# A two-layer decoder trunk on one core: most tile transposes go from TensorE to VectorE and a crossing through memory

## The chip, the core and the metric

The kernel runs on one core of a Trainium2 chip. A core has TensorE (PE), VectorE (DVE), ScalarE (ACT), GpSimd (POOL) and SyncE (SP), each with an instruction queue of its own that it works through in order, and 16 DMA engines. The metric is device time in microseconds. The profile's "span" is the time from the first to the last recorded work of one execution.

## What is computed

Two decoder layers on 256 tokens of width 2048, in float32. In each layer the input projection has seven parts (q, k, v, g_att, glu_a, glu_b, g_conv); one head group does attention, the other a convolution module, and one output projection brings both back to the residual stream.

```python
def conformer_conv(glu_a, glu_b, dw_kernel, dw_bias, ln_g, ln_b, w_pw):
    u = glu_a * jax.nn.sigmoid(glu_b)
    u = jnp.pad(u, ((0, 0), (CONV_WIDTH - 1, 0), (0, 0)))
    y = lax.conv_general_dilated(u, dw_kernel.astype(u.dtype)[:, None, :], window_strides=(1,),
                                 padding="VALID", dimension_numbers=("NWC", "WIO", "NWC"),
                                 feature_group_count=D_CONV) + dw_bias
    y = jax.nn.silu(layer_norm(y, ln_g, ln_b))
    return jnp.einsum("bsc,ce->bse", y, w_pw)
...
for layer in range(DEPTH):
    h = rms_norm(x, norm_g[layer])
    proj = jnp.einsum("bsd,de->bse", h, w_in[layer])
    q, k, v, g_att, glu_a, glu_b, g_conv = jnp.split(proj, SPLIT_POINTS, axis=-1)
    q = apply_rope(rms_norm(q.reshape(B, S, N_HEADS, HEAD_DIM), q_norm_g[layer]), cos, sin)
    k = apply_rope(rms_norm(k.reshape(B, S, N_HEADS, HEAD_DIM), k_norm_g[layer]), cos, sin)
    att = dilated_mixture(q, k, v).reshape(B, S, D_ATT)
    att_y = rms_norm(att, att_out_g[layer]) * jax.nn.silu(g_att)
    conv = conformer_conv(glu_a, glu_b, dw_kernel[layer], dw_bias[layer], conv_ln_g[layer],
                          conv_ln_b[layer], w_pw[layer])
    conv_y = rms_norm(conv, conv_out_g[layer]) * jax.nn.silu(g_conv)
    x = x + jnp.einsum("bse,ed->bsd", jnp.concatenate([att_y, conv_y], axis=-1), w_out[layer])
```

## The kernel before

**Weight tiles.** Each projection is cut into groups of 512 output columns, and each group into 8 weight tiles of 256 rows (512 KB). A layer has 320 tiles in a fixed order: for j = 0 to 3 the groups glu_b, glu_a, v, q, k (tiles 0 to 159), then g_conv 0, g_att 0 to 3, g_conv 1 to 3 (160 to 223), o_att 0 to 3 (224 to 255), pw 0 to 3 (256 to 287) and o_conv 0 to 3 (288 to 319). Layer 1 has the same, 320 later. A tile is loaded on SyncE's queue into one of `R_RAW` buffers (line 224), split into a high half by ScalarE (line 238) and a low half by VectorE (line 239), both into one of `R_SPLIT` = 4 buffers, three tiles ahead (`AHEAD`), and used in 12 products (line 669): high by high, low by high, high by low, for two row blocks and two token blocks. The other operand stands in `st_hi[s][c]` and `st_lo[s][c]`, four chunks c of 512 channels: s = 0 for the layer's input and later for the attention's result, s = 1 for the convolution's.

**Side work and its place.** All other work of a layer is written as generators whose steps begin with a `Need(...)`: PSUM banks, a condition, and the time they take on an engine. While the program is recorded, the `Filler` keeps a clock for each engine (P, V, A, G) and after each weight tile emits, by priority, the steps that fit within a horizon (4.5 us for VectorE, 3.5 for ScalarE). A step that fits nowhere waits for a later tile. Before a tile whose operand is not there yet, `fill.until` emits what is left of the work that it needs, whether it fits or not. So the order on every engine is fixed when the program is built, and each engine works through it in that order.

**The side work that the text speaks of.** `transposes` (line 280) turns a tile of 256 tokens by 512 channels with eight TensorE transposes into two banks; 44 such sets stand in the program (glu_a, q and k for each j; g_att, pw and the next layer's input through `to_stationary`). `conv` computes 31 taps for four chunks on VectorE (lines 403 and 406), two instructions of 128x256 to a step, with the lowest priority, and at its end GpSimd adds the channels' sums (`ysum`, lines 412 and 414). After the fourth chunk comes `layer_norm`: a product with ones (line 422), the mean (424, ScalarE), its subtraction (432, VectorE), squares (435, ScalarE), their sum in eight pieces (355 and 357, GpSimd), a product with ones (366), a copy (369), the power -0.5 and a spread copy (271, 272, 441, GpSimd), a product that turns it (445), a copy (447), the multiplication (455, VectorE), silu (458, ScalarE), and the high and low halves (461, 462). Its result is the first operand of pw, `st_hi[1]` and `st_lo[1]`, read first by tile 256 (576 in layer 1). `rope_tables` (lines 631, 634, 636) builds four tables on GpSimd, each with one table load, two small loads and a multiplication; the one for layer 1 is written out at the last tile of o_att 3 of layer 0.

## Time and profile before

| | |
|---|---|
| median of 3 runs | 1853.98 us (1853.09 to 1854.18) |
| the profiled execution | 1854.28 us, of it the span 1852.5 us |
| busy in the span | PE 1844.7, DVE 1397.7, ACT 987.4, POOL 142.3 us |
| DMA | 349.97 MB, mean 189 GB/s |
| granted TensorE clock | 9 tenths or more in all 40 slices |

The page's fourth part follows the chain of work that ended last; where it lies on one engine nearly throughout, that engine's work sets the time and the others only matter where it waits for them. A timeline row gives start, duration, engine, line, operation and, in brackets, the idle time before it and what ended it; a row with xN holds N instructions.

### The profile page before, as it was taken

How to read it: one execution, taken by the hardware profiler on the slowest of the kernel's cores; microseconds unless marked ns; L12 is line 12 of the kernel's file. 1: busy time of each engine (PE TensorE's matmuls, PEld its weight loads, DVE VectorE, ACT ScalarE, POOL GpSimd, SP SyncE). 2: the span in 40 equal slices, each digit the busy share in tenths (PEclk: the TensorE clock that was granted, in tenths of full speed). 3: DMA queues.
4: the chain of work that ended last, by engine and by line, in shares of the span. 5: the costliest groups of instructions: out<-in, count | busy, mean ns of one | idle time of the engine just before them, and what ended most of it. 6: DMA issues, size and time to landing. Idle time of an engine off the chain costs nothing.

```text
span 1852.5 us, 23729 instructions
## 1 busy us (share of the span) xinstructions
PE 1844.7 (100%) x8494; PEld 1534.4 (83%) x8494; DVE 1397.7 (75%) x2162; ACT 987.4 (53%) x1549; POOL 142.3 (8%) x153
## 2 busy tenths in 40 slices
PE   9999999999999999999999999999999999999999
PEld 6888888888888888888888888888888888888887
DVE  6888889788889876555558888797887998755554
ACT  6465564655644465445444655646556445644542
POOL 0210100200010140000000101002001002100000
PEclk9999999999999999999999999999999999999999
DMA  8655656556566676555666556565565666665564
GB/s 276 211 183 162 189 157 197 183 161 192 162 191 194 193 221 210 194 183 196 208 202 193 183 162 191 159 194 181 161 192 160 194 195 190 213 204 195 176 205 146
DMA packets 180599, 349.97 MB, mean 189 GB/s; under 512 B 11216, under 2 KB 11216, under 8 KB 180480
## 3 DMA queue, kind: packets, MB, share of 16 engines
q1 hardware_dynamic: 178512, 345.09, 59.6%
q0 software_dynamic: 960, 1.77, 0.5%
q8 instruction: 66, 1.08, 0.2%
q10 hardware_dynamic: 1008, 1.59, 0.2%
q14 instruction: 53, 0.43, 0.1%
HBM read 344.21 MB, written 4.19 MB: 188 GB/s over the span
## 4 chain that ended last, share of the span: by engine, by line
PE 99%; DMA 0%; DVE 0%; ACT 0%; ACTq 0%; issue 0%
PE acc L669 94%; PE ax L280 2%; PE ax L517 1%; PE ax L534 1%; PE ax L543 0%; PE ax L542 0%; PE ax L541 0%; PE ax L516 0%; DMA y<-in_x_t 0%; PE ax L366 0%; DVE wlo L239 0%; PE ax L445 0%; PE ax L422 0%; DVE stlo L307 0%; DVE a L602 0%; ACT whi L249 0%
## 5 line engine op out<-in xcount | busy, mean ns | idle before, releaser
L239 DVE TENSOR_TENSOR wlo<-raw,whi 128x1024 fp32r<-128x1024 f32 x639 | 792.0, 1248 | 392.2 <-ACT whi L238 386.0
L238 ACT ACTIVATE whi<-raw 128x1024 fp32r<-128x1024 f32 x639 | 674.6, 1063 | 658.1 <-PE acc L669 480.6
L669 PE MATMUL acc<-whi,sthi 128*128 128x512 f32 x2560 | 822.6, 392 | 2.0 <-ACT whi L249 2.0
L669 PE MATMUL acc<-wlo,sthi 128*128 128x512 f32 x2560 | 814.9, 389 | 0.3 <-DVE wlo L239 0.3
L669 PE MATMUL acc<-whi,stlo 128*128 128x512 f32 x2560 | 814.7, 389 | 0.0
L669 PEld LDWEIGHTS acc<-wlo,sthi 128*128 128x128 f32 x2560 | 480.4, 188 | 101.7 <-DVE wlo L250 0.9
L669 PEld LDWEIGHTS acc<-whi,stlo 128*128 128x128 f32 x2560 | 480.6, 188 | 100.4
L669 PEld LDWEIGHTS acc<-whi,sthi 128*128 128x128 f32 x2560 | 475.8, 188 | 98.0 <-ACT whi L249 3.3
L406 DVE SCALAR_TENSOR_TENSOR y<-ut,prm,y 128x256 f32<-128x256 f32 x960 | 410.1, 485 | 0.0
L414 POOL TENSOR_TENSOR ysum<-ysum,y 128x256 f32<-128x256 f32 x30 | 36.6, 1218 | 240.9 <-DVE y L406 131.6
L479 POOL TENSOR_SCALAR qr<-qss 128x8 f32<-128x8 f32 x16 | 3.1, 197 | 663.7 <-ACT junk L476 663.7
L476 ACT ACTIVATE junk<-acc,rx 128x128 bf16<-128x128 f32 x128 | 47.0, 367 | 8.4 <-PE acc L669 4.8
L486 ACT ACTIVATE d<-acc,qr 128x128 f32<-128x128 f32 x128 | 34.7, 383 | 16.9 <-POOL qr L481 16.9
L291 ACT ACTIVATE sthi<-ax,prm 128x256 fp32r<-128x256 f32 x64 | 25.1, 475 | 30.7 <-PE ax L280 30.7
L293 DVE SCALAR_TENSOR_TENSOR stlo<-ax,prm,sthi 128x256 fp32r<-128x256 f32 x64 | 26.5, 475 | 14.4 <-ACT sthi L291 14.4
L507 ACT ACTIVATE c<-ax 128x512 f32<-128x512 f32 x32 | 17.4, 596 | 33.7 <-PE ax L280 33.7
L530 ACT ACTIVATE sm<-sm,smm 128x128 f32<-128x128 f32 x64 | 28.2, 442 | 6.6 <-DVE smm L525 6.6
L357 POOL TENSOR_TENSOR ssum<-ssum,d 128x512 f32<-128x512 f32 x14 | 28.5, 2036 | 6.5 <-ACT d L435 5.6
L480 POOL TENSOR_TENSOR qr<-qr,half 128x8 f32<-128x8 f32 x16 | 26.3, 1643 | 1.3
L280 PEld LDWEIGHTS ax<-ident,d 128*128 128x128 f32 x192 | 22.4, 140 | 3.2
L280 PE MATMUL ax<-ident,d 128*128 128x128 f32 x192 | 24.9, 273 | 0.0
L476 ACT ACTIVATION_READ_ACCUMULATOR junk<-acc,rx 128x1 f32 x128 | 24.7, 193 | 0.0
(112 smaller groups left out, 666.7 us busy)
## 6 DMA issues: line engine op xcount, KB each, us to landing
raw<-in_w_in SPq DMA_DIRECT2D x447, 512.0 KB, 3.8
raw<-in_w_out SPq DMA_DIRECT2D x128, 512.0 KB, 4.7
raw<-in_w_pw SPq DMA_DIRECT2D x64, 512.0 KB, 4.7
a<-in_x SPq DMA_DIRECT2D x4, 512.0 KB, 5.7
xs<-a SPq DMA_DIRECT2D x4, 512.0 KB, 6.7
a<-xs SPq DMA_DIRECT2D x4, 512.0 KB, 5.6
y<-in_x_t SPq DMA_DIRECT2D x3, 512.0 KB, 7.2
out<-a SPq DMA_DIRECT2D x4, 256.0 KB, 4.9
```

Source lines behind the costliest of these rows:

```text
L238: S.activation(hi, a, AF.Copy)
L239: V.tensor_sub(wlo[i % R_SPLIT], a, hi.bitcast(F32))
L280: T.transpose(banks[b][:, i * SEQ + tt * 128:i * SEQ + tt * 128 + 128], src[:, tt, e:e + 128], ident)
L293: V.scalar_tensor_tensor(st_lo[s][c][:, i], p[i], gain(i), st_hi[s][c][:, i].bitcast(F32), op0=ALU.mult, op1=ALU.subtract)
L357: G.tensor_add(ssum, ssum, half_sq)
L406: V.scalar_tensor_tensor(y[:, c], u[:, c, k:k + SEQ], w[:, c, l * CW + k:l * CW + k + 1], y[:, c], op0=ALU.mult, op1=ALU.add)
L414: G.tensor_add(ysum, ysum, y[:, c])
L476: S.activation(junk[:, :DH], ps[tt][:, h * DH:(h + 1) * DH], AF.Square, scale=rx[:, tt:tt + 1], accum_out=qss[:, tt, h:h + 1])
L480: G.tensor_tensor(qr, qr, half.rearrange("p (t h) -> p t h", t=2), op=ALU.pow)
L486: S.activation(n[:, tt, h * DH:(h + 1) * DH], ps[tt][:, h * DH:(h + 1) * DH], AF.Copy, scale=qr[:, tt, h:h + 1])
L530: S.activation(s[:, cs], s[:, cs], AF.Exp, bias=m[:, tt:tt + 1], scale=-1.0, accum_out=lsum[:, tt:tt + 1])
L669: T.matmul(ps[tt], xl if n == 2 else xh, lo[:, kk] if n == 1 else hi[:, kk], start=(k == 0 and n == 0), stop=(k == KT - 1 and n == 2))
```

## The change

Of the 44 sets of eight transposes, 41 no longer run on TensorE. `turn` lets VectorE transpose the 32x32 blocks inside a tile (two instructions of 128x512 into one buffer, `blocks`), writes the result to a buffer in memory, and reads it back in four transfers so that each lands as a transposed tile, with its tokens in another order. Readers take it through a view (`turned`): ScalarE's copies to the convolution's input and to q, the products of `head` for k, and eight low-half instructions of 128x128 instead of four of 128x256 in `to_stationary_turned`. A lock, held while the program is recorded, admits one set to `blocks` at a time. A new clock Q in the planner gives the write 8 us and the reads 9 us; the steps behind them are placed when these are over. The last chunk of pw in each layer and the last chunk of layer 1's input stay on TensorE. There are five raw weight buffers instead of four, the fifth load and one input load stand elsewhere in the code, and the descriptor scratch is set to 4096.

```diff
-R_RAW, R_SPLIT = 4, 4
+R_RAW, R_SPLIT = 5, 4
...
-        self.t = dict(P=0.0, V=0.0, A=0.0, G=0.0)
+        self.t = dict(P=0.0, V=0.0, A=0.0, G=0.0, Q=0.0)
...
-            if n == 0 and ready > (now if e == "P" else max(now, self.t[e]) + 0.2):
+            if n == 0 and ready > (now if e in "PQ" else max(now, self.t[e]) + 0.2):
...
-    qT, kT = (C[i].rearrange("p (h s) -> p h s", h=4) for i in (1, 2))
+    qT, kT = C[1].rearrange("p (h s) -> p h s", h=4), C[2]
...
+    blocks = t([128, 2 * CH], "blocks")
...
+    crossing = [dr.tile([4, 128, SEQ], F32, name=f"crossing{i}") for i in range(2)]
+    turns = [0, False]
...
+    def turn(src, dst):
+        yield Need(0, lambda: not turns[1], V=1.4)
+        turns[1] = True
+        for tt in range(2):
+            V.transpose(blocks.rearrange("p (b c t j) -> p t c b j", b=4, c=4, t=2)[:, tt],
+                        src[:, tt].rearrange("p (c b j) -> p c b j", c=4, b=4))
+        yield Need(Q=8.0)
+        way = crossing[turns[0] % 2]
+        turns[0] += 1
+        nc.sync.dma_start(way.rearrange("b p x -> p b x"), blocks.rearrange("p (b x) -> p b x", b=4))
+        yield Need(Q=9.0)
+        turns[1] = False
+        for a in range(4):
+            nc.sync.dma_start(dst[:, a * SEQ:(a + 1) * SEQ], way[:, 32 * a:32 * a + 32])
+    def turned(z):
+        return z.rearrange("p (a c t j) -> p c t a j", a=4, c=4, t=2)
+    def to_stationary_turned(src, dst, s, c, gain):
+        yield from turn(src, dst)
+        yield Need(0, lambda: vacant[s][c], A=1.8, V=2.2)
+        z = turned(dst)
+        hi, lo = (o[s][c].rearrange("p c (t a j) -> p c t a j", t=2, a=4) for o in (st_hi, st_lo))
+        for i in range(4):
+            S.activation(hi[:, i], z[:, i], AF.Copy, scale=gain(i))
+        for i in range(4):
+            for tt in range(2):
+                V.scalar_tensor_tensor(lo[:, i, tt], z[:, i, tt], gain(i), hi[:, i, tt].bitcast(F32),
+                                       op0=ALU.mult, op1=ALU.subtract)
+        filled(s, c)
...
-        yield from to_stationary(A[c], 0, c, lambda i: ng[:, l * KT + 4 * c + i:l * KT + 4 * c + i + 1])
+        gain = lambda i: ng[:, l * KT + 4 * c + i:l * KT + 4 * c + i + 1]
+        if c < NCH - 1:
+            yield from to_stationary_turned(A[c], Y[c], 0, c, gain)
+        else:
+            yield from to_stationary(A[c], 0, c, gain)
...
-        yield Need(2, has("conv", l, j - 2) if j >= 2 else None, P=0.9)
-        banks = [fill.bank(), fill.bank()]
-        transposes(Dt[0], banks)
-        yield Need(A=1.0)
-        for b in range(2):
-            S.activation(uT[j % 2][:, 2 * b:2 * b + 2, PAD:], banks[b].rearrange("p (c s) -> p c s", c=2), AF.Copy)
-        fill.free(*banks)
+        z = Dt[0].rearrange("p t e -> p (t e)")
+        yield from turn(Dt[0], z)
+        yield Need(0, has("conv", l, j - 2) if j >= 2 else None, A=1.7)
+        for c in range(4):
+            S.activation(uT[j % 2][:, c, PAD:].rearrange("p (t a j) -> p t a j", t=2, a=4), turned(z)[:, c], AF.Copy)
...
-        yield Need(2, has("qk", l, j - 1) if j else None, P=0.9)
-        banks = [fill.bank(), fill.bank()]
-        transposes(o, banks)
+        before = has("qk", l, j - 1) if j else None
+        if nm == "q":
+            z = o.rearrange("p t e -> p (t e)")
+            yield from turn(o, z)
+            yield Need(0, before, A=1.8)
+            for h in range(4):
+                S.activation(qT[:, h].rearrange("p (t a j) -> p t a j", t=2, a=4), turned(z)[:, h], AF.Copy)
+        else:
+            yield Need(0, before)
+            yield from turn(o, kT)
         flag("rope", l, j, nm)
-        yield Need(A=1.0)
-        dst = qT if nm == "q" else kT
-        for b in range(2):
-            S.activation(dst[:, 2 * b:2 * b + 2], banks[b].rearrange("p (h s) -> p h s", h=2), AF.Copy)
-        fill.free(*banks)
+        yield Need()
...
-        T.matmul(ps[:, 0:128], qT[:, h, 0:128], kT[:, h, 0:128], start=True, stop=True)
-        T.matmul(ps[:, 128:384], qT[:, h, 128:256], kT[:, h, 0:256], start=True, stop=True)
+        k = turned(kT)[:, h]
+        T.matmul(ps[:, 0:128], qT[:, h, 0:128], k[:, 0], start=True, stop=True)
+        T.matmul(ps[:, 128:384], qT[:, h, 128:256], k, start=True, stop=True)
...
-        yield from to_stationary(A[j], 0, j, lambda i: prm[:, 4 * j + i, P_ATT + l:P_ATT + l + 1])
+        yield from to_stationary_turned(A[j], A[j].rearrange("p t e -> p (t e)"), 0, j,
+                                        lambda i: prm[:, 4 * j + i, P_ATT + l:P_ATT + l + 1])
...
-        yield from to_stationary(y, 1, j, lambda i: prm[:, 4 * j + i, P_CONV + l:P_CONV + l + 1])
+        gain = lambda i: prm[:, 4 * j + i, P_CONV + l:P_CONV + l + 1]
+        if j < NCH - 1:
+            yield from to_stationary_turned(y, Y[j], 1, j, gain)
+        else:
+            yield from to_stationary(y, 1, j, gain)
...
+    load(4)
...
     split_first()
+    x_load(3)
...
-            if a == 1:
-                x_load(3)
...
-    nc = bacc.Bacc("TRN2", target_bir_lowering=False, num_devices=1)
+    nc = bacc.Bacc("TRN2", target_bir_lowering=False, num_devices=1, dynamic_dma_scratch_size=4096)
```

The order of four engines shows what moves, each of before and then of after. In the names, numbers at the end tell buffers apart: y_81 to y_84 are the four convolution chunks, a_85 to a_88 the residual chunks, sthi_65 to sthi_68 the operand of o_att, sthi_69 to sthi_72 that of pw, acc the accumulators, whi and wlo the split buffers.

TensorE at the end of o_att 3 and the start of pw 0 in layer 0, before:

```order
L669 MATMUL acc_156<-whi_96,sthi_68 128x512
L669 MATMUL acc_156<-wlo_100,sthi_68 128x512
L669 MATMUL acc_156<-whi_96,stlo_76 128x512
L669 MATMUL acc_156<-whi_96,sthi_68 128x512
L669 MATMUL acc_156<-wlo_100,sthi_68 128x512
L669 MATMUL acc_156<-whi_96,stlo_76 128x512
L669 MATMUL acc_153<-whi_93,sthi_69 128x512
L669 MATMUL acc_154<-whi_93,sthi_69 128x512
L669 MATMUL acc_153<-wlo_97,sthi_69 128x512
L669 MATMUL acc_154<-wlo_97,sthi_69 128x512
```

and after:

```order
L720 MATMUL acc_158<-whi_97,stlo_76 128x512
L720 MATMUL acc_158<-whi_97,sthi_68 128x512
L720 MATMUL acc_158<-wlo_101,sthi_68 128x512
L720 MATMUL acc_158<-whi_97,stlo_76 128x512
L410 MATMUL ax_161<-ones,ssum 128x2 x4
L487 MATMUL ax_162<-ident,rbc 128x128 x2
L720 MATMUL acc_155<-whi_94,sthi_69 128x512
L720 MATMUL acc_156<-whi_94,sthi_69 128x512
L720 MATMUL acc_155<-wlo_98,sthi_69 128x512
L720 MATMUL acc_156<-wlo_98,sthi_69 128x512
```

The two small products of the layer norm (with ones and with the identity), which stood some 25 tiles earlier, now stand between o_att's last and pw's first product; it is the same in layer 1.

GpSimd from the convolution's last sums on, layer 0, before:

```order
L414 TENSOR_TENSOR ysum<-ysum,y_84 128x256 x4
L355 COPY ssum<-d_108 128x512
L357 TENSOR_TENSOR ssum<-ssum,d_108 128x512
L357 TENSOR_TENSOR ssum<-ssum,d_109 128x512 x2
L357 TENSOR_TENSOR ssum<-ssum,d_108 128x512 x2
L357 TENSOR_TENSOR ssum<-ssum,d_109 128x512 x2
L271 TENSOR_SCALAR rstd<-rsc 128x2
L272 TENSOR_TENSOR rstd<-rstd,half 128x2
L441 COPY rbc<-rstd 128x256
L631 DMA ropeqa<-in_rope_cos 128x2x128
L634 DMA gbc<-in_q_norm_g 128x64 x2
```

and after:

```order
L456 TENSOR_TENSOR ysum<-ysum,y_84 128x256 x4
L683 DMA ropeqa<-in_rope_cos 128x2x128
L686 DMA gbc<-in_q_norm_g 128x64 x2
L688 TENSOR_TENSOR ropeqa<-ropeqa,gbc 128x256
L683 DMA ropeqb<-in_rope_sin 128x2x128
L686 DMA gbc<-in_q_norm_g 128x64 x2
L688 TENSOR_TENSOR ropeqb<-ropeqb,gbc 128x256
L683 DMA ropeka<-in_rope_cos 128x2x128
L686 DMA gbc<-in_k_norm_g 128x64 x2
L688 TENSOR_TENSOR ropeka<-ropeka,gbc 128x256
L683 DMA ropekb<-in_rope_sin 128x2x128
L686 DMA gbc<-in_k_norm_g 128x64 x2
```

The sum of squares follows only behind the fourth rope table, and with it the power and the spread copy.

VectorE round the last convolution step of layer 0, before:

```order
L406 SCALAR_TENSOR_TENSOR y_84<-ut_102,prm,y_84 128x256 x4
L239 TENSOR_TENSOR wlo_99<-raw_91,whi_95 128x1024
L406 SCALAR_TENSOR_TENSOR y_84<-ut_102,prm,y_84 128x256 x2
L239 TENSOR_TENSOR wlo_100<-raw_92,whi_96 128x1024
L239 TENSOR_TENSOR wlo_97<-raw_89,whi_93 128x1024
L239 TENSOR_TENSOR wlo_98<-raw_90,whi_94 128x1024
L239 TENSOR_TENSOR wlo_99<-raw_91,whi_95 128x1024
L239 TENSOR_TENSOR wlo_100<-raw_92,whi_96 128x1024
L432 TENSOR_TENSOR y_81<-y_81,nmean 128x1024
L432 TENSOR_TENSOR y_82<-y_82,nmean 128x1024
```

and after:

```order
L243 TENSOR_TENSOR wlo_99<-raw_92,whi_95 128x1024
L448 SCALAR_TENSOR_TENSOR y_84<-ut_103,prm,y_84 128x256 x2
L243 TENSOR_TENSOR wlo_100<-raw_93,whi_96 128x1024
L243 TENSOR_TENSOR wlo_101<-raw_89,whi_97 128x1024
L243 TENSOR_TENSOR wlo_98<-raw_90,whi_94 128x1024
L243 TENSOR_TENSOR wlo_99<-raw_91,whi_95 128x1024
L243 TENSOR_TENSOR wlo_100<-raw_92,whi_96 128x1024
L629 SCALAR_TENSOR_TENSOR a_88<-acc_157,ra,a_88 128x512
L629 SCALAR_TENSOR_TENSOR a_88<-acc_158,ra,a_88 128x512
L474 TENSOR_TENSOR y_81<-y_81,nmean 128x1024
L474 TENSOR_TENSOR y_82<-y_82,nmean 128x1024
L474 TENSOR_TENSOR y_83<-y_83,nmean 128x1024
```

The last step stood behind the split of tile 214 and stands now behind that of tile 253; five splits and the evacuation of o_att 3 (line 629) come before the subtractions of the mean. In layer 1 the last step stands behind the split of tile 572, and the subtractions behind that of tile 577 and ahead of the evacuation.

ScalarE at pw's start, layer 0, before:

```order
L447 ACTIVATE nmean<-ax_160 128x256
L238 ACTIVATE whi_95<-raw_91 128x1024
L238 ACTIVATE whi_96<-raw_92 128x1024
L458 ACTIVATE y_81<-y_81,prm 128x256 x4
L461 ACTIVATE sthi_69<-y_81 128x1024
L238 ACTIVATE whi_93<-raw_89 128x1024
L458 ACTIVATE y_82<-y_82,prm 128x256 x4
L238 ACTIVATE whi_94<-raw_90 128x1024
L461 ACTIVATE sthi_70<-y_82 128x1024
```

and after:

```order
L489 ACTIVATE nmean<-ax_162 128x256
L500 ACTIVATE y_81<-y_81,prm 128x256 x4
L500 ACTIVATE y_82<-y_82,prm 128x256 x4
L503 ACTIVATE sthi_69<-y_81 128x1024
L242 ACTIVATE whi_97<-raw_93 128x1024
L242 ACTIVATE whi_94<-raw_89 128x1024
L500 ACTIVATE y_83<-y_83,prm 128x256 x4
L500 ACTIVATE y_84<-y_84,prm 128x256 x4
L503 ACTIVATE sthi_70<-y_82 128x1024
```

The first two chunks' silus now stand together, and the splits of tiles 259 and 260 (whi_97 and whi_94) stand between the first operand of pw and the silus of the other two.

## Rows read from the trace of the kernel before

**Rows 1.** Chain of the page, by engine and line (share of the span):
```profile
PE acc L669 94%; PE ax L280 2%; PE ax L517 1%; PE ax L534 1%; PE ax L543 0%; PE ax L542 0%; PE ax L541 0%; PE ax L516 0%; DMA y<-in_x_t 0%; PE ax L366 0%; DVE wlo L239 0%; PE ax L445 0%; PE ax L422 0%; DVE stlo L307 0%; DVE a L602 0%; ACT whi L249 0%
```

**Rows 2.** TensorE's timeline round one set of transposes (start us, us, engine, line, operation):
```profile
641.53 1.03 PE L280 MATMUL ax<-ident,a 128*128 128x128 f32 x8
...
642.87 0.62 PE L669 MATMUL acc<-wlo,sthi 128*128 128x512 f32 x2
...
643.33 0.63 PE L669 MATMUL acc<-whi,stlo 128*128 128x512 f32 x2
```

**Rows 3.** Costliest groups of the page: busy us, mean ns, idle time before them:
```profile
L239 DVE TENSOR_TENSOR wlo<-raw,whi 128x1024 fp32r<-128x1024 f32 x639 | 792.0, 1248 | 392.2 <-ACT whi L238 386.0
L238 ACT ACTIVATE whi<-raw 128x1024 fp32r<-128x1024 f32 x639 | 674.6, 1063 | 658.1 <-PE acc L669 480.6
...
L406 DVE SCALAR_TENSOR_TENSOR y<-ut,prm,y 128x256 f32<-128x256 f32 x960 | 410.1, 485 | 0.0
```

**Rows 4.** Groups of VectorE by line and shape, columns as in rows 3:
```profile
L495 DVE TENSOR_TENSOR d<-d,ropeka 128x512 f32<-128x512 f32 x16 | 11.0, 685 | 0.0
...
L455 DVE TENSOR_TENSOR y<-y,nmean 128x1024 f32<-128x1024 f32 x8 | 9.6, 1218 | 0.0
```

**Rows 5.** Busy time by engine in one stretch (columns PE, PEld, DVE, ACT, POOL, clock, DMA):
```profile
108.00:215.00 107.00, 107.00 (x508) 89.65 (x507) 92.66 (x167) 58.22 (x97) 6.95 (x7) 1.00 0.59 178
```

**Rows 6.** DMA queue and DMA issues of the page:
```profile
q1 hardware_dynamic: 178512, 345.09, 59.6%
...
raw<-in_w_in SPq DMA_DIRECT2D x447, 512.0 KB, 3.8
```

**Rows 7.** GpSimd's timeline, 590 to 735 us:
```profile
626.10 2.52 POOL L414 TENSOR_TENSOR ysum<-ysum,y 128x256 f32<-128x256 f32 x2 [0.43 <-DVE y L406]
...
644.74 0.61 POOL L355 COPY ssum<-d 128x512 f32<-128x512 f32 x1 [16.11 <-ACT d L435]
...
645.43 10.26 POOL L357 TENSOR_TENSOR ssum<-ssum,d 128x512 f32<-128x512 f32 x5
...
658.46 4.40 POOL L357 TENSOR_TENSOR ssum<-ssum,d 128x512 f32<-128x512 f32 x2 [2.77 <-ACT d L435]
...
672.28 0.19 POOL L271 TENSOR_SCALAR rstd<-rsc 128x2 f32<-128x2 f32 x1 [9.42 <-DVE rsc L369]
...
673.33 0.40 POOL L441 COPY rbc<-rstd 128x256 f32<-128x256 f32 x1
...
673.66 0.80 POOL L631 DMA_DIRECT2D ropeqa<-in_rope_cos  x1
...
701.49 0.76 POOL L636 TENSOR_TENSOR ropekb<-ropekb,gbc 128x256 f32<-128x256 f32 x1 [3.69 <-DMA gbc<-in_k_norm_g]
```

**Rows 8.** Line 357 alone: ns min/median/max, first and last start:
```profile
L357 POOL TENSOR_TENSOR ssum<-ssum,d x14: 1297/2158/2170, 645.4 to 1581.4; 128x512 f32<-128x512 f32 x14
```

**Rows 9.** VectorE's timeline, 643 to 700 us:
```profile
646.36 4.56 DVE L239 TENSOR_TENSOR wlo<-raw,whi 128x1024 fp32r<-128x1024 f32 x2
...
672.04 0.15 DVE L369 COPY rsc<-ax 128x2 f32<-128x2 f32 x1
```

**Rows 10.** TensorE's timeline, two places (1590 to 1592 and 678 to 683 us):
```profile
1590.35 0.95 PE L366 MATMUL ax<-ones,ssum 128*128 128x2 f32 x8
...
681.39 0.61 PE L445 MATMUL ax<-ident,rbc 128*128 128x128 f32 x4
```

**Rows 11.** ScalarE's timeline, 634 to 646 and 679 to 692 us:
```profile
643.60 1.07 ACT L435 ACTIVATE d<-y 128x1024 f32<-128x1024 f32 x1
...
682.04 0.38 ACT L447 ACTIVATE nmean<-ax 128x256 f32<-128x256 f32 x1 [2.11 <-PE ax L445]
...
687.12 2.08 ACT L458 ACTIVATE y<-y,prm 128x256 f32<-128x256 f32 x4 [1.28 <-DVE y L455]
...
689.23 1.06 ACT L461 ACTIVATE sthi<-y 128x1024 fp32r<-128x1024 f32 x1
```

**Rows 12.** TensorE's timeline, 0 to 7 us:
```profile
1.44 4.45 PE L615 MATMUL acc<-junk 128*128 128x512 bf16 x10 [1.44 <-DVE junk L612]
```

## The prediction

> **What bounds the kernel now.** I read the page's chain first, then TensorE's timeline round one set of transposes, then the costliest groups, and last GpSimd's timeline round the layer norm. The chain that ended last lies on TensorE: 94% of the span are the main products of line 669, 2% the transposes of line 280, and most of the rest is its small products [rows 1]. So every microsecond off TensorE shortens the kernel, as long as TensorE never has to wait, and every wait put ahead of it is paid in full. A pair of products takes 0.46 us (642.87 to 643.33) [rows 2], so a weight tile, twelve products, takes 2.76 us. ScalarE and VectorE split each tile: 1.06 and 1.25 us, and both wait mostly for TensorE to free a buffer (481 us of ScalarE's idle time ends on a product, 386 us of VectorE's on ScalarE's split) [rows 3]. With four split buffers, the split of tile n can begin once TensorE enters tile n-3. That ties the other engines' programs to TensorE's, and lets me put times on the order shown above.
>
> **What the change takes off.** Eight transposes stand between 641.53 and 642.87 together with one pair of products: 1.34 less 0.46 is 0.88 us of TensorE [rows 2]. There are 44 such groups, 38.7 us, which agrees with the chain's 2% [rows 1]. 41 of them go (328 of 352 transposes by the order, where the words of the change say 296 of 320; three groups stay, one for pw in each layer and one for the input of layer 1): 41 x 0.88 = 36.1 us. It cannot be more than this.
>
> **What it adds beside TensorE.** Each set needs two VectorE transposes of 128x512; none is in this trace, and the nearest row is a 128x512 product at 0.69 us [rows 4], so 1.4 us per set (bounds 1.4 to 2.8). The low halves come as eight pieces of 128 in place of four of 256 (such a piece takes 0.485 [rows 3]): between nothing and 1.9 us more, I take 0.7. Over one layer's 20 sets that is some 40 us of VectorE. In a stretch full of the convolution VectorE is busy for 92.66 of 107 us [rows 5], so there is room for it, but the convolution, which fills what is left, is pushed back. ScalarE's share hardly changes (k's copies go, the others come as four instead of two). The crossing adds 42 MB to 350 MB; the queue's transfers take 59.6% of the engines' time now [rows 6], some 70% then, beside TensorE's work. The fifth raw tile gives the loads, which land in 3.8 us [rows 6], one tile more of slack; it and the earlier loads I cost at nothing, since TensorE waits for no load now.
>
> **What is moved: the layer norm.** This is where the time goes. In the order before, the last convolution step stands after the split of tile 214, in the order after behind that of tile 253, three tiles from the end of o_att. The sums over channels (line 366) and the spread of the result (line 445) were queued on TensorE some 25 tiles ahead of pw; now both stand directly before pw's first product. The order of TensorE is fixed, so the whole chain from the last convolution step to pw's first operand, less what o_att still covers, becomes a standstill of TensorE, once per layer.
>
> Layer 0: the split of tile 253 begins when TensorE enters tile 250, six tiles or 16.6 us before o_att's end. ScalarE 1.06, VectorE 1.25, two conv instructions 2 x 0.485 [rows 3]: the convolution ends 13.3 us before o_att does. Its last sums on GpSimd take 2.5 us (626.10 to 628.62) [rows 7]: 10.8 before. Next on GpSimd now stands the block of layer 1's rope tables, which before stood behind the norm. It ran from 673.66 to 702.25, 28.6 us, nearly all of it waits for its own small transfers [rows 7]: it ends 17.8 us after TensorE has stopped. Then the eight pieces of the squares' sum: 0.61 and seven adds. An add took between 1.30 and 2.16 us [rows 8]; at 644.74 to 655.69 and 658.46 to 662.86 they ran at the slow value, beside VectorE's splits, of which a pair took 4.56 us there [rows 9] against 2 x 1.25. In the standstill VectorE has nothing to do, so I take 0.61 + 7 x 1.30 = 9.7 us, with 15.3 (0.61 + 10.26 + 4.40) as the upper bound. [...] The rest of the chain: sums on TensorE 0.95 [rows 10], a copy 0.15 [rows 9], GpSimd's power and copy 1.45 (672.28 to 673.73) [rows 7], the spread 0.6 [rows 10], its copy 0.38, VectorE's product 1.22 [rows 4], two sets of silu, as ScalarE's order now puts them, 2 x 2.08, the copy to the high half 1.06 [rows 11], 0.3 for the low half, and eight handovers of about 0.1: 11.1 us. Layer 0 stands for 17.8 + 9.7 + 11.1 = 38.6 us (36 to 45).
>
> Layer 1 has no rope block. There the convolution ends after split 572, early enough, and what comes last is the subtraction of the mean, which VectorE's order puts behind the split of tile 577. That starts two tiles, 5.5 us, before the end; with 1.06 + 1.25 + 1.22 and a square of 1.07 [rows 11] the sums start 0.8 us before TensorE stops. Sums 11.5 (one split and three subtractions still run beside them; 9.7 to 15.3), and 11.1: 21.8 us (19 to 26).
>
> Three smaller costs. ScalarE's order puts split 260 ahead of the second pair of silus, and that split waits for TensorE's tile 256: 2.76 + 1.06 + 2 x 2.08 + 1.06 + 0.4 = 9.4 us after pw begins, when TensorE is there after 5.5. A second wait of 3.9 us per layer, 7.8 (5 to 10). [...] I take 2 us for each restart, 4 in all (0 to 8). The crossings: a write waits two tiles, reads three, and their readers another three, 8.2 us by 2.76; for reads that land now and then behind that, 4 us (0 to 25).
>
> **Sum.** Against the profiled execution's 1854.28 us, which lies 0.3 above the median of the runs: 1854.3 - 36.1 + 38.6 + 21.8 + 7.8 + 4 + 4 = 1894.4, so 1895 us.
>
> **Rivals.** First, faster: the norm still hides behind o_att, and only the gain is left, 1854.3 - 36.1 + 4 = 1822 us. It decides at one place: the chain of layer 0 is 2.5 + 28.6 + 9.7 + 11.1 = 52 us long, so the convolution would have to end 19 tiles before o_att does, against five. For it speaks that VectorE had 13% free in the full stretch [rows 5]; against it that VectorE works in program order and may not pass the splits, which wait for TensorE. Even with the rope block out of the way both layers would stand some 22 us, more than is gained. I give it 4%; within 0.2% of before (0.2% is about what a measurement of this kernel can tell from no change), with the stalls at about half, 3%.
>
> Second, the crossing's reads land late. A packet of the queue took 59.6% x 16 x 1852.5 / 178512 = 99 ns [rows 6]. A set's reads are 512 pieces of 1 KB; over 16 engines they need 1.6 to 3.2 us, and all is hidden. If few engines took them, four for example, 128 pieces each at 49 to 99 ns make 6.3 to 12.7 us, in which loads queue behind them; the loads have some 7 us to spare, so a set would cost nothing at the lower end and 5 us at the upper. I take 2 us x 41 = 80: 1975. For it speaks the order of the view that is read (4, 32, 256), against it the waits left in the order. [...] 12%.
>
> Third, VectorE's transposes take twice what I took, 2.8 us per set. 28 us more per layer in stretches with 13% free pushes the convolution back by some 15 to 20 us per layer, and both standstills grow by it: 1930. 6%.
>
> **How the numbers follow.** The sum as worked out, 75%, runs from 1868 (38.7 off, were a group's gain as large as 0.94; 36 + 19 + 5 on, less 8 for a rope block whose transfers land sooner) to 1935 (45 + 26 + 10 + 8 + 25 on, 33 off, were it 0.8). The third rival lies within this; the second and the first, 16%, are mostly left out. So 1868 to 1938. Faster by over 0.2%: 4%; within: 3%; slower: 93%.
>
> **What would show it.** In the profile after: two gaps on TensorE, some 39 us at the end of layer 0's o_att and 22 at that of layer 1, with line 487 or the first pw product behind them, and shorter ones one chunk later; GpSimd's rope block at a place ahead of the squares' sums, which then run at 1.30 us; line 284 with six groups in place of 44; VectorE's transposes near 0.7 us; the reads landing within 8 us. TensorE busy throughout would prove the first rival; waits on ScalarE's copies of the turned tiles, spread over all stages, the second; a convolution that ends after o_att, the third.

## The result, and the profile after

The changed kernel takes 1974.26 us (median of 4 runs, 1972.87 to 1974.95) against 1854.08 for the kernel before: 1.065 times as long, 95% interval 1.0636 to 1.0663. The forecast was slower, at 1895 us within 1868 to 1938: the direction held, the size did not. Some 80 us were missing. The second rival, reads that land late, had given 1975 us at a chance of 12%; its cause will be found, but not its price.

The page of the changed kernel: span, busy time of two engines, the granted clock in 40 slices, the DMA queue, the chain, and the first operation it adds.

```profile
span 1972.3 us, 23517 instructions
...
PE 1849.0 (94%) x8166; PEld 1520.8 (77%) x8166; DVE 1439.8 (73%) x2312; ACT 988.9 (50%) x1565; POOL 130.9 (7%) x153
...
PEclk9999999999999998799999999999999999988999
...
q1 hardware_dynamic: 221808, 388.09, 63.7%
...
PE 75%; DMA 7%; ACT 6%; DVE 5%; issue 4%; POOL 3%; SPq 1%; ACTq 0%; POOLq 0%; DVEq 0%
...
L294 DVE STREAM_TRANSPOSE blocks<-d 128x512 f32<-128x512 f32 x48 | 31.1, 688 | 0.0
```

Where the chain lay on TensorE alone [rows 1], a quarter of it now runs over other engines and transfers. VectorE's transpose costs 0.69 us, what the nearest row said [rows 4]. TensorE's work should have gone down by 36 us, but it is busy for 1849.0 us, 4 more than before: part of its products run at the lower clock (granted 0.50 in place of 1.00, see below). The two dips in the clock row lie at the two standstills ahead of pw and the restarts behind them.

TensorE's timeline of the changed kernel shows where it stands. These are the rows with idle time ahead of them (in brackets) that count most, layer 0 and then layer 1.

```profile
146.22 0.79 PE L720 MATMUL acc<-whi,sthi 128*128 128x512 f32 x1 [6.10 <-ACT d L528]
...
793.93 1.87 PE L410 MATMUL ax<-ones,ssum 128*128 128x2 f32 x8 [23.63 <-POOL ssum L401]
797.59 1.23 PE L487 MATMUL ax<-ident,rbc 128*128 128x128 f32 x4 [1.80 <-POOL rbc L483]
805.58 1.22 PE L720 MATMUL acc<-whi,sthi 128*128 128x512 f32 x2 [6.76 <-ACT sthi L503]
...
817.11 0.74 PE L720 MATMUL acc<-whi,sthi 128*128 128x512 f32 x2 [2.96 <-ACT sthi L503]
...
1770.90 1.86 PE L410 MATMUL ax<-ones,ssum 128*128 128x2 f32 x8 [12.19 <-POOL ssum L401]
1774.55 1.22 PE L487 MATMUL ax<-ident,rbc 128*128 128x128 f32 x4 [1.79 <-POOL rbc L483]
1782.54 1.22 PE L720 MATMUL acc<-whi,sthi 128*128 128x512 f32 x2 [6.76 <-ACT sthi L503]
1794.04 0.73 PE L720 MATMUL acc<-whi,sthi 128*128 128x512 f32 x2 [3.28 <-ACT sthi L503]
```

All rows but the first are the two standstills at pw that the forecast was about, with the second waits one chunk later: 59.2 us of idle time. The first row is one of eight of its kind, one for each j in each layer, which the forecast did not have. The waits of the changed kernel give their sum and what lies behind them (us in total, times, longest):

```profile
PE acc L720 <- ACT d L528: 48.8, 16, 6.3
...
ACT c L548 <- DMA d<-crossing: 39.5, 8, 5.4
ACT ut L432 <- DMA d<-crossing: 36.9, 6, 7.0
...
ACT sthi L316 <- DMA y<-crossing: 30.8, 5, 8.1
```

Line 528 is the copy on ScalarE that empties the accumulators of q and k, here those of k; TensorE needs them for the second group after k. Line 548 copies q's turned tile. How the one leads to the other stands in ScalarE's timeline of the changed kernel, 125 to 150 us,

```profile
135.51 1.34 ACT L548 ACTIVATE c<-d 128x256 f32<-128x256 f32 x4 [5.18 <-DMA d<-crossing]
...
137.71 0.35 ACT L518 ACTIVATE junk<-acc,rx 128x128 bf16<-128x128 f32 x1
...
145.02 2.18 ACT L528 ACTIVATE d<-acc,qr 128x128 f32<-128x128 f32 x8 [1.54 <-POOL qr L523]
```

and in SyncE's queue over the same time (start, time for the issue):

```profile
123.89 2.45 SPq L303 DMA_DIRECT2D d<-crossing  x4
126.38 18.94 SPq L228 DMA_DIRECT2D raw<-in_w_in  x6
```

The four reads are issued from 123.89 to 126.34 us and let ScalarE go at 135.51: 11.6 us after the first, 9.2 after the last issue. ScalarE has waited 5.18 us by then. Only behind this copy come k's squares (line 518), the power on GpSimd, and k's copies, and at 146.22 TensorE gets its accumulators, 6.1 us late. In the kernel before, k's squares did not wait for anything but TensorE; its ScalarE timeline has

```profile
119.77 0.37 ACT L476 ACTIVATE junk<-acc,rx 128x128 bf16<-128x128 f32 x1 [0.30 <-PE acc L669]
```

directly behind k's last product. In the code, `ev_qk` lets k begin when the flag `rope` of q is up; before, that flag stood behind eight transposes on TensorE, now it stands behind a write, four reads and the copies that read them.

Each gap has a second price. Busy time and granted clock (the column behind POOL's) of the changed kernel in stretches round the first of the eight gaps:

```profile
130.00:140.00 10.00, 10.00 (x45) 8.06 (x43) 4.04 (x6) 4.69 (x16) 0.00 (x0) 1.00 0.59 176
140.00:146.00 6.00, 0.12 (x1) 0.00 (x0) 3.44 (x5) 4.36 (x14) 3.08 (x3) 0.72 0.45 117
146.00:149.00 3.00, 2.54 (x5) 1.75 (x6) 2.47 (x6) 3.00 (x8) 0.00 (x0) 0.50 0.78 293
...
152.00:155.00 3.00, 3.00 (x13) 2.37 (x13) 1.56 (x2) 1.06 (x1) 0.00 (x0) 0.86 0.46 161
```

During the gap the granted clock falls from 1.00 to 0.50, and it is back at 1.00 only some 6 us after TensorE has begun again; a pair of products takes 0.86 us in between (147.84 to 148.70) in place of 0.46. The pair's 1024 columns in 0.86 us are 1.2 a nanosecond; it is such stretches, with a granted clock of 0.50, that the expectations below call 1.2 GHz. So this gap costs some 3 us more. Behind the other seven, 3.5 to 6.2 us of products ran at 0.50.

### The profile page after: what moved, and what is told of

Same layout as the page of the kernel before. It is cut to its first block, busy times and chain, and to the rows that moved or that the text cites. A ratio compares the mean times of both kernels' runs of the same rounds, so it can differ in the third digit from the quotient of the medians.

```text
span 1972.3 us, 23517 instructions
## 1 busy us (share of the span) xinstructions
PE 1849.0 (94%) x8166; PEld 1520.8 (77%) x8166; DVE 1439.8 (73%) x2312; ACT 988.9 (50%) x1565; POOL 130.9 (7%) x153
## 4 chain that ended last, share of the span: by engine, by line
PE 75%; DMA 7%; ACT 6%; DVE 5%; issue 4%; POOL 3%; SPq 1%; ACTq 0%; POOLq 0%; DVEq 0%
PE acc L720 71%; DVE y L448 3%; DMA y<-crossing 2%; ACT whi L242 2%; DMA raw<-in_w_in 1%; DMA d<-crossing 1%; ACT junk L518 1%; DVE wlo L243 1%; DMA c<-crossing 1%; POOL ssum L401 1%; ACT d L528 1%; ACT y L500 1%; SPq L303 1%; PE ax L563 1%; POOL qr L522 1%
## 5 line engine op out<-in xcount | busy, mean ns | idle before, releaser
L243 DVE TENSOR_TENSOR wlo<-raw,whi 128x1024 fp32r<-128x1024 f32 x639 | 783.1, 1232 | 414.4 <-ACT whi L242 386.5
L720 PE MATMUL acc<-whi,sthi 128*128 128x512 f32 x2560 | 834.1, 397 | 70.7 <-ACT d L528 48.8
L720 PE MATMUL acc<-wlo,sthi 128*128 128x512 f32 x2560 | 824.2, 393 | 2.2 <-DVE wlo L243 2.2
L720 PE MATMUL acc<-whi,stlo 128*128 128x512 f32 x2560 | 823.6, 393 | 0.0
L720 PEld LDWEIGHTS acc<-whi,sthi 128*128 128x128 f32 x2560 | 486.3, 191 | 180.6 <-ACT d L528 56.2
L456 POOL TENSOR_TENSOR ysum<-ysum,y 128x256 f32<-128x256 f32 x30 | 30.7, 1025 | 482.7 <-DVE y L448 367.3
L432 ACT ACTIVATE ut<-d 128x256 f32<-128x256 f32 x32 | 11.1, 408 | 41.0 <-DMA d<-crossing 36.9
L294 DVE STREAM_TRANSPOSE blocks<-d 128x512 f32<-128x512 f32 x48 | 31.1, 688 | 0.0
L548 ACT ACTIVATE c<-d 128x256 f32<-128x256 f32 x32 | 10.7, 407 | 39.5 <-DMA d<-crossing 39.5
L571 DVE CUSTOM_DVE_ANT_0 sm<-ax,mask 128x128 f32<-128x128 f32 x64 | 20.4, 356 | 8.9 <-PE ax L563 8.7
```

The lines of the kernel that those rows point to most:

```text
L243: V.tensor_sub(wlo[i % R_SPLIT], a, hi.bitcast(F32))
L294: V.transpose(blocks.rearrange("p (b c t j) -> p t c b j", b=4, c=4, t=2)[:, tt], src[:, tt].rearrange("p (c b j) -> p c b j", c=4, b=4))
L456: G.tensor_add(ysum, ysum, y[:, c])
L571: V.tensor_tensor_reduce(s[:, cs], ps[:, cs], mask[:, cs], -1.0, 3e38, op0=ALU.add, op1=ALU.min, accum_out=m[:, tt:tt + 1])
L720: T.matmul(ps[tt], xl if n == 2 else xh, lo[:, kk] if n == 1 else hi[:, kk], start=(k == 0 and n == 0), stop=(k == KT - 1 and n == 2))
```

## The experiments

Theory A after these readings has three parts. The reads land late, because their view of 4 by 32 rows spreads them badly over the DMA engines; k's evacuation, now emitted behind the crossing, passes that on to TensorE; and the layer norm stands exposed as forecast. The rival to the first is that the queue is simply full, to the second that ScalarE is held in any case, to the third that something else at pw is slow.

**e1_read16.** The buffer in memory gets another layout: written in four transfers of 32 partitions, read in four transfers of 128 rows that lie one behind the other.

```diff
-        nc.sync.dma_start(way.rearrange("b p x -> p b x"), blocks.rearrange("p (b x) -> p b x", b=4))
+        for a in range(4):
+            nc.sync.dma_start(way[a].rearrange("(b r) x -> r b x", r=32),
+                              blocks[32 * a:32 * a + 32].rearrange("p (b x) -> p b x", b=4))
...
-            nc.sync.dma_start(dst[:, a * SEQ:(a + 1) * SEQ], way[:, 32 * a:32 * a + 32])
+            nc.sync.dma_start(dst[:, a * SEQ:(a + 1) * SEQ], way[a])
```

> The changed kernel with another layout of the buffer in memory: the tile is written in four transfers of 32 partitions each, and each read then takes 128 rows that lie one behind the other, in place of a view of 4 by 32 rows. Bytes, order on the engines and waits stay the same. Theory A (the reads land late because their view lets them use few of the 16 engines, and ScalarE, waiting for them, holds back the evacuation that frees TensorE's accumulators): ScalarE's waits on the crossing (107 us in lines 548, 432 and 316 together) fall under 15 us, the eight gaps of some 6 us on TensorE in front of a product released by line 528 go, and with them the stretches at 1.2 GHz behind them: 1974 - 48 - 26 = about 1900 us, 1890 to 1910. Theory B (the reads are late because they queue behind the weight loads on one queue that is busy for 64%): nothing gets earlier, 1965 to 1985 us.

Measured: 1921.06 us (1917.44 to 1922.12), 53 less than the changed kernel; the ratio to before is 1.0356 (1.0339 to 1.0373). ScalarE's waits on the crossing in those three lines are down to 10.4 us in place of 107. Here are what is left of TensorE's waits at k's evacuation, and the larger part of ScalarE's 10.4:

```profile
PE acc L722 <- ACT d L530: 15.0, 16, 1.3
...
ACT ut L434 <- DMA d<-crossing: 9.0, 5, 2.4
```

So the layout is the cause of the lateness, not the load on the queue: the same bytes, behind the same weight loads, land in time. (The write has changed too, but the last packet of q's write ends at 122.26 us in the changed kernel and the reads are issued from 123.89, so that the 11.6 us above are the reads' own.) The time stays above the 1910 of theory A, because k's evacuation still comes 1.9 us too late eight times, with reads that are early: the second part of the theory works without the first.

**e8_read_pairs.** The opposite: each read cut in two reads of 2 by 32 rows.

```diff
-            nc.sync.dma_start(dst[:, a * SEQ:(a + 1) * SEQ], way[:, 32 * a:32 * a + 32])
+            for h in range(2):
+                nc.sync.dma_start(dst[64 * h:64 * h + 64, a * SEQ:(a + 1) * SEQ], way[2 * h:2 * h + 2, 32 * a:32 * a + 32])
```

> The changed kernel with each read of 4 by 32 rows cut in two reads of 2 by 32 rows into 64 partitions: the same bytes in twice as many transfers, 8 for a tile in place of 4. Theory A (a read uses as many engines as its view's slowest dimension has entries, four now, and two then): the same 512 pieces take twice as long, some 18 us from the issue to ScalarE's copy in place of 9, the gaps in front of k's evacuation grow by about 9 us each and loads are held too: 2050 us or more. Theory B (it is the number of bytes, their layout in memory, or the queue that makes the reads late): about as now, 1970 to 1990.

Measured, in a single run: 2166.74 us, over the 2050 of theory A. The waits show that the weight loads are late as well now, which they hardly were in the changed kernel (24.5 us of VectorE's waits, as in e1), and that the gap at k's evacuation has nearly doubled, by 5.7 us where 9 were expected. (The copy of q's tile, line 549, waits for its reads; they are put down to a load that landed last.)

```profile
PE acc L721 <- ACT d L529: 94.0, 16, 11.9
...
ACT whi L242 <- DMA raw<-in_w_in: 64.4, 23, 10.5
ACT c L549 <- DMA raw<-in_w_in: 63.5, 6, 11.0
```

Its queue at the same place, and ScalarE's copy of q's tile:

```profile
132.01 7.41 SPq L304 DMA_DIRECT2D d<-crossing  x8
...
148.65 1.33 ACT L549 ACTIVATE c<-d 128x256 f32<-128x256 f32 x4 [10.18 <-DMA raw<-in_w_in]
```

From the first issue to the copy it is 16.6 us, in place of 11.6. That goes theory A's way, but the run doubles the number of transfers too, and their issue alone takes 7.41 us in place of 2.45.

The packets in the three traces separate the two. The reads of a set are 512 packets of 1 KB, and a packet takes 46 ns (median) in all three. What differs is how many are under way at a time, on average over a set's reads: 4.0 in the changed kernel, 8.2 in e1, 2.1 here (medians of 41 sets). From the first packet's start to the last one's end a set takes 7.2, 3.0 and 12.4 us. So the pieces are not slower where the view begins with few, and fewer of them run side by side; e8's later issue comes on top. Which engines took them no row names, so theory A is shown as far as the packets go: 4.0, 2.1 and 8.2 at a time through views that begin with 4, 2 and 128.

**e6_k_early.** The changed kernel, with k's squares and copies waiting only for q's rotation, and k's rotation for q's tile:

```diff
-        before = ("rope", l, j, "q") if nm == "k" else ("rope", l, j - 1, "k") if j else None
+        before = ("roped", l, j) if nm == "k" else ("rope", l, j - 1, "k") if j else None
...
-            yield Need(V=1.9)
+            yield Need(0, has("rope", l, j, "q") if nm == "k" else None, V=1.9)
...
         if nm == "q":
+            flag("roped", l, j)
```

> The changed kernel with only that condition changed; the reads stay late, the convolution's steps and the rope tables as they are. By the order, k's evacuation stands 6 tiles earlier, the convolution ends 5 tiles earlier (248, 568), and the rope block stands behind the first pieces of the squares' sum. Theory A (the late reads cost TensorE time only by way of k's evacuation, emitted at the last moment): the eight gaps go, 48 us and 26 us of products at 1.2 GHz, and the standstills shrink by the 5 tiles' 13 us per layer: 1974 - 74 - 20 = 1880 us, 1865 to 1900. Theory B (late reads hold ScalarE, and with it the splits, wherever they stand): the gaps come back in front of products that wait for splits, and the time stays above 1925.

Measured: 1960.00 us (1959.37 to 1966.84), only 14 less. Theory A as I had put it falls, and theory B holds in its time (over 1925) but not in its place. The eight gaps in front of line 528 are gone, and eight others have come, in front of products that read the turned tile and not of those that wait for splits:

```profile
PE ax L563 <- DMA c<-crossing: 37.4, 8, 5.9
...
PE ax L410 <- POOL ssum L401: 31.0, 2, 26.1
```

Line 563 is the first product of q and k, which reads k's tile straight from the crossing. It is queued on TensorE some four tiles behind the reads; they landed 9.9 us after the last issue here as well. So the late reads have two ways to TensorE, and closing one opens the other. (In layer 0 the rope block now stands inside the squares' sum: the wait for it is 26.1 us although the convolution ends five tiles earlier.)

**e2_rope_late.** The changed kernel with the rope tables of layer 1 built after pw 3:

```diff
-            if nm == "o_att" and j == NCH - 1 and l + 1 < DEPTH:
+            if nm == "pw" and j == NCH - 1 and l + 1 < DEPTH:
```

> The changed kernel with the rope tables of layer 1 built after pw 3 instead of after o_att 3, so that on GpSimd they no longer stand ahead of the squares' sum. Theory A (in layer 0 the sum waits for the rope block): the gap of 23.6 us on TensorE before line 410 in layer 0 shrinks to that of layer 1, about 12 us, and the time falls by 11 to 13 us, to about 1962. Theory B (the sum is bound by the end of the convolution and the chain behind it, and the rope block fits beside it): no change, 1972 to 1976.

Measured: 1964.87 us (1963.82 to 1966.94), 9.4 less. TensorE's gap before line 410 in layer 0 shrinks from 23.6 to 15.6 us, not to 12. GpSimd's timeline of this run, and VectorE's row ahead of it, tell why:

```profile
771.39 4.62 DVE L474 TENSOR_TENSOR y<-y,nmean 128x1024 f32<-128x1024 f32 x4
...
773.76 2.72 POOL L399 COPY ssum<-d 128x512 f32<-128x512 f32 x1 [13.82 <-ACT d L477]
776.56 9.30 POOL L401 TENSOR_TENSOR ssum<-ssum,d 128x512 f32<-128x512 f32 x7
```

With the rope block away, the next in line is the square, and that waits for the subtraction, which VectorE's order puts behind the evacuation of o_att 3, that is behind the end of TensorE's work. Only 10.1 us (783.87 in the changed kernel against 773.76) could be won, and the first copy gives 2.1 of them back: beside VectorE's subtractions it takes 2.72 us, where it took 0.60 in the changed kernel.

**e3_conv_early.** One number of the planner: a step of the convolution is put down at less time, so that more steps are emitted between the splits.

```diff
-                    yield Need(V=0.8)
+                    yield Need(V=0.65)
```

> The changed kernel with one number of the planner changed: a step of the convolution is put down at 0.65 us of VectorE instead of 0.8, so that more steps go between the splits. By the order, the convolution then ends behind the split of tile 227 in place of 253 (547 in place of 572), and the norm's last small product on TensorE stands 14 tiles ahead of pw in both layers. Theory A (the late end of the convolution exposes the norm): the first group of pw, 66 and 52 us now against 22 before, falls to 22 to 24 in both layers, 1974 - 44 - 30 = 1900 us, up to 1915 if VectorE falls behind the splits here and there. Theory B (VectorE has no room, the steps put earlier delay the splits): TensorE waits for splits all along the first 227 tiles, and the gain is under half of this, 1940 or more.

Measured: 1903.81 us (1901.87 to 1906.23), 70 less, as theory A had it. VectorE had the room; no wait on the norm is left among this run's waits on TensorE, and the eight gaps at k's evacuation stay:

```profile
PE acc L720 <- ACT d L528: 50.3, 16, 7.0
```

**e4_all_three** is e1, e2 and e3 together.

> All three together: reads of 128 rows, rope tables after pw 3, convolution steps at 0.65 us. If the three causes are independent and complete, what is left is the gain on TensorE: 1854 - 36 + 5 = 1823 us, 1815 to 1840, faster than the kernel before. If the removed transposes were worth less than 0.88 us a set, or the turned tiles cost something not yet seen, it ends above 1845.

Measured: 1839.77 us (1838.63 to 1842.70), 0.9926 times the kernel before (0.9912 to 0.9941). It is 21 us above what e5 will show: 14.0 in one line of its waits, k's evacuation once more, and 8.0 in slower products (TensorE busy for 1816.8 us against 1808.8; behind three of the gaps the products slow down, and 10.0 us of them go at some 0.86 us a pair).

```profile
PE acc L722 <- ACT d L530: 14.0, 16, 2.0
```

**e5_best** is e4 with the edit of e6.

> The kernel of run e4_all_three with one condition changed: k's squares and normalising copies on ScalarE, which free k's accumulators, no longer wait (in the planner) for q's tile to be back from memory, only for q's rotation to have read its input; the wait for q's tile moves to k's rotation on VectorE. By the order, k's evacuation then stands 6 tiles earlier, and the convolution ends behind the split of tile 216 in place of 227. Theory A (k's evacuation is emitted only when TensorE needs its accumulators, because the crossing delays q): the eight gaps of 0.5 to 2 us on TensorE and the slow products behind them go, 13 us with a few us of lower clock: 1840 - 13 - 4 = 1823 us, 1818 to 1830. Theory B (the rest of e4 is lower clock or other costs of the turned tiles): 1836 to 1842.

Measured: 1818.37 us (median of 5, 1818.31 to 1818.84), 0.9809 times the kernel before (0.9796 to 0.9823). Its page:

```profile
span 1817.1 us, 23689 instructions
...
PE 1808.8 (100%) x8166; PEld 1500.0 (83%) x8166; DVE 1445.1 (80%) x2312; ACT 987.8 (54%) x1565; POOL 145.7 (8%) x153
...
PEclk9999999999999999999999999999999999999999
```

1854.3 less 36.1 is 1818.2. With the waits out of the way TensorE is busy for 35.9 us less than before, where 36.1 were counted from one set; the medians of this kernel and of the one before, run beside it, lie 35.4 us apart (1853.75).

**e7_before_planner.** The other side: the kernel before with five raw buffers, the moved loads, the late rope tables and a convolution step at 0.65, and all its transposes on TensorE.

> The kernel before, with what else has been touched but no transposes moved: five raw buffers, the loads where the changed kernel has them, rope tables after pw 3, a convolution step at 0.65 us. Theory A (these alone bring nothing, since TensorE waits for nothing in the kernel before; the gain of e4 and e5 is that of the transposes): 1854 us, 1851 to 1857. Theory B (part of e4's gain is the planner's): under 1850.

Measured: 1854.62 us (1853.81 to 1855.13), ratio 1.0004 (0.9995 to 1.0013). The gain of e5 is that of the transposes; the rest only makes room for it, and the fifth buffer, the loads and the scratch setting cost nothing that the interval tells from zero.

**e9_norm_undone** and **e10_read4_undone** take one cause at a time back into e5: the first puts the convolution's step and the rope tables back as in the changed kernel, the second the reads and the write.

> The kernel of run e5_best with the two edits round the layer norm taken back: a convolution step at 0.8 us again, the rope tables at o_att 3. Reads of 128 rows and k's early evacuation stay. By the order, the convolution ends behind the splits of tiles 248 and 568, and the norm's two small products stand before pw's first product. Theory A (the norm's price is independent of the reads): the same gaps as in run e6_k_early at pw, 54 us in all, and some 12 us of products at 1.2 GHz behind them: 1818 + 66 = 1884 us, 1870 to 1895. Theory B (with reads that land early the rest of the program takes up part of it): under 1860.

> The kernel of run e5_best with the reads through the view of 4 by 32 rows again, and the write in one transfer. Theory A (late reads are paid at the first product of q and k, as in run e6_k_early, where the gaps before it were 37 us, besides what the reads of the turned tiles for the next layer and of pw cost, and each gap has some 3 us of products at 1.2 GHz behind it): 1818 + 37 + 10 + 25 = 1890 us, 1875 to 1905. With e9 the two then add up to e6: 66 + 72 over 1818 is 1956, against 1960 measured. Theory B (late reads matter only together with the late norm): under 1850.

Measured: 1884.55 us (1884.01 to 1886.21) and 1893.34 (1889.15 to 1894.19). The late norm costs 66 us, the late reads 75; added to 1818 they give 1959, and e6, which has both, takes 1960. So in these kernels the two prices simply add. TensorE's waits of e9 and then of e10:

```profile
PE ax L412 <- POOL ssum L403: 31.3, 2, 26.4
...
PE acc L723 <- ACT sthi L505: 19.8, 4, 6.8
```

```profile
PE ax L563 <- DMA c<-crossing: 23.3, 7, 5.6
...
PE acc L721 <- DVE wlo L243: 15.1, 11, 3.5
```

In e10 a part of the price is paid as late splits, spread over eleven places; ahead of the first, ScalarE had waited 7.1 us for q's turned tile, and its splits stand behind that copy.

## Why the prediction was right and wrong

With e5 as the kernel without waits the changed kernel's time can be split. Against before, TensorE lost 36 us of transposes (1808.8 busy in e5 against 1844.7) and gained 40.2 us of slower products (1849.0 against 1808.8, the same instructions). Idle time: 59.2 us at pw, 48.8 at k's evacuation, 4.5 at layer 1's last input chunk, 2.8 before splits. -36 + 40.2 + 59.2 + 48.8 + 4.5 + 2.8 = 119.5; the spans differ by 119.8.

- **The gain**, 36.1 us: right, 35.9 of TensorE's busy time, as e5 shows. (Line 284 is left with 24 transposes, three sets, as counted in the sum; the six groups named as a sign were wrong.)
- **The standstill in layer 0**, 38.6 us: 35.3 measured (TensorE stops at 770.3, the first product of pw starts at 805.58). GpSimd's timeline of the changed kernel confirms it link by link:

```profile
757.42 2.52 POOL L456 TENSOR_TENSOR ysum<-ysum,y 128x256 f32<-128x256 f32 x2 [0.43 <-DVE y L448]
759.89 0.80 POOL L683 DMA_DIRECT2D ropeqa<-in_rope_cos  x1
...
783.19 0.72 POOL L688 TENSOR_TENSOR ropekb<-ropekb,gbc 128x256 f32<-128x256 f32 x1 [2.72 <-DMA gbc<-in_k_norm_g]
783.87 0.60 POOL L399 COPY ssum<-d 128x512 f32<-128x512 f32 x1
784.55 9.33 POOL L401 TENSOR_TENSOR ssum<-ssum,d 128x512 f32<-128x512 f32 x7
```

  The channel sums end 10.4 us before the stop (10.8 forecast); the rope block takes 24.0 us (28.6, as in [rows 7]; this is what made the standstill shorter); the squares' sum takes 10.0 (9.7 forecast, with the fast value taken because VectorE would be idle); the chain behind it 11.7 (11.1). An add takes 1.3 us here (9.33 for seven), beside an idle VectorE, against a median of 2.16 in the kernel before [rows 8], where VectorE's splits ran beside the sum [rows 9]; e2's copy, 2.72 us beside VectorE's subtractions against 0.60, goes the same way.
- **The standstill in layer 1**, 21.8 us: 23.8 measured. **The second waits**, 3.9 each: 2.96 and 3.28.
- **The restarts**, 2 us each: too small, and my estimate alone; no run shows this figure. What they show is more: e9, which has these standstills and no late reads, keeps TensorE busy for 1822.0 us, 13.2 more than e5, where I had 4 (0 to 8). I priced one slow start for each standstill, after the kernel's first products [rows 12]. Two things were missing, as the granted clock of the changed kernel shows (columns as above):

```profile
806.00:811.00 5.00, 5.00 (x13) 3.84 (x13) 1.92 (x2) 0.48 (x1) 0.00 (x0) 0.50 0.32 95
812.00:817.00 5.00, 2.15 (x10) 1.43 (x8) 1.23 (x1) 5.00 (x11) 0.00 (x0) 1.00 0.35 105
...
819.00:821.00 2.00, 2.00 (x6) 1.57 (x5) 0.45 (x1) 0.00 (x0) 0.00 (x0) 0.50 0.13 22
```

  The first slow stretch is longer: the granted clock stays at 0.50 from 774.1 to 811.6 us, which takes in 6.0 us of pw's products and the norm's small ones before them. And each standstill is followed by the second wait, after which the clock falls to 0.50 once more, from 818.5 to 821.9 us.
- **The crossing**, 4 us (0 to 25): this step failed. In the split above it is the 48.8, 4.5 and 2.8 us of idle time and the 27.0 us of slower products that the standstills of e9 don't account for, some 83 us; the late reads alone cost 75 in e10. I gave the readers of the turned tiles 8.2 us, the three tiles by which the order sets them behind the reads, and took for granted that the reads would mostly make that. They need 11.6. The longer time stood in the few-engines rival, 6.3 to 12.7 us for the pieces (7.2 measured), and was left at 12%, although no row spoke for the shorter one: the trace of before has no transfer with such a view, so nothing in it showed that the view's order decides. The rival had the cause of the lateness right, as far as the packets show it (4.0 under way at a time, 8.2 in e1, 2.1 in e8), and its 1975 us is close to the 1974 measured, but that is luck: it let loads queue for 2 us in each of the 41 sets, and by its own working pieces that take 7.2 us would have cost next to nothing. What was paid is eight gaps of 6 us, each with some 3 us of slower products, and loads hardly ran late.
- **What was not looked at**: who waits for the wait that is added. The flag that lets k be evacuated moved behind q's crossing, and in the order k's squares went from behind the split of tile 42 to that of tile 48. The order was read at pw and not here. With reads that land in time this alone costs 21 us (e4 against e5). The kernel of e9 is the changed one with both put right, the reads and k's place in the order: 1884.55 us, 90 less than the changed kernel and within the range of the forecast.
- **The third rival**, slow transposes on VectorE: refuted, 0.69 us each. **The first**, a hidden norm: refuted as argued; e3 shows that the convolution's end decides it.
- **The range**: its upper end took 25 us for the crossing. That bound was not worked out from rows, and it broke by some 58 us; the restarts' bound of 8 broke too, by 5.

## What to carry to other kernels

When an operation moves from an engine that is always on time to a chain of transfers, list every flag and buffer that its end released, and look in the order at where each of those waiters now stands; the transfer's own lateness is only a part of the price. In an order fixed beforehand, extra work on an engine that has room can still cost dearly, because it pushes the lowest priority back until its result is needed: here a planner's cost of 0.65 instead of 0.8 us took 70 us off. And the outer count of a transfer's view was part of its price here: with 4 in front the reads of a set took 7.2 us, with 128 they took 3.0. So before a change rests on a transfer, try the rows arranged so that the side that is read begins with many.

## What the runs showed of the hardware

The same 512 KB, read in four transfers, let ScalarE go 11.6 us after the first issue when the view began with 4, and made it wait no more than 2.4 us, where it waited at all, when it began with 128; cut into eight transfers with views that begin with 2 it took 16.6 us, and weight loads behind it kept ScalarE waiting for up to 10.5 us. A packet of 1 KB took 46 ns (median) in all three; 4.0, 8.2 and 2.1 of them were under way at a time. A stop of 5.2 to 6.3 us on TensorE was followed by 3.5 to 6.4 us of products at a granted clock of 0.50 (0.86 us a pair against 0.46). GpSimd's add of 128x512 takes 1.26 us beside an idle VectorE (least and median of 14 in the changed kernel) and up to 2.13 beside a busy one.
